# When to make the operand sums of a seven-product matmul: beside the transposes, or four pairs later

## The chip, the cores and the metric

One core of a Trainium2 chip runs the whole program in one launch. The metric is the device time of that launch in microseconds (us); lower is better. TensorE (PE) does the matrix products, VectorE (DVE) and ScalarE (ACT) the elementwise work, and SyncE (SP) issues the loads from HBM. Each of these executes its own instructions in a fixed order that is written when the program is built.

## The reference

A decoder trunk of two layers on 256 tokens of width 2048, all in float32. Each layer has attention and then a dense MLP with a hidden width of 8192:

```python
for layer in range(DEPTH):            # DEPTH = 2
    ...                               # projections, self- and memory attention
    h = layer_norm(ALPHA * h + mix, ln_g[layer, 0], ln_b[layer, 0])
    ffn = jnp.square(jax.nn.relu(h @ w_up[layer])) @ w_down[layer]
    h = layer_norm(ALPHA * h + ffn, ln_g[layer, 1], ln_b[layer, 1])
```

The change lies in the two products of the MLP.

## The kernel before

**Precision.** Every float32 operand is split into two parts, hi (`split`, L96, a cast on ACT) and lo (L97, a subtraction on DVE). One product of a 128-token block with a weight block of 128 x 512 takes three matmuls: hi by hi (L254), lo weights (L255) and lo tokens (L256).

**The MLP.** The hidden width is cut into four chunks of 2048. A chunk consists of two W_up groups (loop variable `v_`), then two W_down groups. A group (`mlp_group`) has 1024 output columns and a contraction over 2048 rows, which is taken as eight *pairs* of 128 rows in the order `ORDER = (2, 3, 0, 4, 1, 5, 6, 7)`. A pair needs one load of 1 MB. An ordinary pair is eight products, 24 matmuls. Pairs 0 and 1, which stand third and fifth in the order, are done with seven products instead (a Strassen-Winograd scheme), 21 matmuls. So a group is 6 x 24 + 2 x 21 = 186 matmuls.

Two groups are done another way, through `aform` and with eight products throughout: the first W_up group of the second layer, and in each layer the second W_down group of the last chunk. All eight second W_up groups (four chunks, two layers) go through `mlp_group`.

**What a seven-product pair needs.** On the weights' side `fast_weights` loads the pair, splits the blocks B11 and B22, and B21, and makes four sums T1 to T4 on DVE (L116, L119, L120), which are split too. On the tokens' side `fast_acts` makes four sums of the token blocks for pairs 0 and 1 at once: it adds hi and lo back together (L129), does four operations of 256 elements (L133 to L136), and splits the 1024 results (one cast on ACT into `sum_g` or `sum_h`, one subtraction on DVE). The sums for W_up (`sum_h`) are made once in a layer, those for W_down (`sum_g`) once in a chunk.

**Buffers.** The loaded weights, the tile t of the weights' sums and the tile `x_f` of the tokens' sums all rotate through four buffers of the tag "raw"; the hi parts have seven buffers of 1024 elements (tag "whi"), the lo parts seven others.

**Order around the change.** When a W_up group is complete, DVE adds the seven-product part, ACT does relu and square (L639 to L641), and the four 128 x 512 blocks must be transposed on PE (`transposed`: four small matmuls, an ACT cast L428, a DVE subtraction L429) to become the tokens of W_down, `gT`. These four transposes are hooks, emitted inside the next group at the places `UHOOKS = ((0, 3), (1, 0), (1, 2), (1, 3))`, where the first number counts pairs in order from 0 and the second the block of outputs within the pair. With the third of them both blocks of `gT0`, which holds the tokens of pairs 0 and 1, are complete, and there the kernel calls `fast_acts`:

```python
def back(b, v_=v_, us=us, gt=gt, sum_g=sum_g):
    transposed(us[b], gt[2 * v_ + b % 2], b // 2, 0)
    if v_ == 0 and b == 2:
        fast_acts(gt[0], sum_g)
```

So `sum_g` is emitted in the second pair of the second W_up group, just ahead of that group's first seven-product pair (the third in order). `sum_h` is emitted ahead of the layer's first `mlp_group`. The order of emission is what the framework's planner starts from when it writes each engine's order; it moves instructions ahead of others where it reckons that an engine is free.

Of the kernel before, what the change touches and what calls it, by code (L numbers as in the profile page):

```python
# [8 lines left out]
F32 = mybir.dt.float32  # L9
F32R = mybir.dt.float32r  # L10
I32 = mybir.dt.int32
AF = mybir.ActivationFunctionType
ALU = mybir.AluOpType
AX = mybir.AxisListType

P = 128
# [9 lines left out]
CH = 2048  # L26
# [7 lines left out]
NRAW = 4  # L34
# [30 lines left out]
WHOOKS = (10, 14, 4)  # L65
NWARM = 2
FILL = (10, 11, 12, 16)
ORDER = (2, 3, 0, 4, 1, 5, 6, 7)
FAST = (0, 1)
UHOOKS = ((0, 3), (1, 0), (1, 2), (1, 3))  # L70
WTAIL = ((1, 2), (2, 0), (3, 1), (5, 2), (7, 1), (9, 2))

# [2 lines left out]
def trunk(ctx: ExitStack, tc: tile.TileContext, a: dict, out: bass.AP):  # L75
    nc = tc.nc
    PS = bass.MemoryType.PSUM
    const = ctx.enter_context(tc.tile_pool(name="const", bufs=1))
    wp = ctx.enter_context(tc.tile_pool(name="wp", bufs=5))
    ap_ = ctx.enter_context(tc.tile_pool(name="act", bufs=1))  # L80
# [14 lines left out]
    def split(hi, lo, src):  # L95
        nc.scalar.copy(hi, src)  # L96
        nc.vector.tensor_tensor(lo, src, hi.bitcast(F32), ALU.subtract)  # L97
# [23 lines left out]
        pair(t_[:, 2:4].rearrange("p q c -> p (q c)"), 1024)  # L121
        return dict(zip(("B11", "B22", "B21", "T1", "T3", "T2", "T4"), tiles))

    def fast_acts(x, s_):


        raw = wp.tile([P, 2048], F32, name="x_f", tag="raw", bufs=NRAW)
        f = raw[:, :1024].rearrange("p (k t) -> p k t", k=4)
        nc.vector.tensor_tensor(f, x[:, :, 0].bitcast(F32), x[:, :, 1].bitcast(F32), ALU.add)  # L129
        a11, a21 = f[:, 0:4:2, :P], f[:, 0:4:2, P:]  # L130
        a12, a22 = f[:, 1:4:2, :P], f[:, 1:4:2, P:]
        s = raw[:, 1024:].rearrange("p (q u t) -> p q u t", q=4, u=2)
        nc.vector.scalar_tensor_tensor(s[:, 0], a21, -1.0, a22, op0=ALU.mult, op1=ALU.subtract)  # L133
        nc.vector.scalar_tensor_tensor(s[:, 1], s[:, 0], -1.0, a11, op0=ALU.mult, op1=ALU.subtract)
        nc.vector.tensor_tensor(s[:, 2], a11, a21, ALU.subtract)
        nc.vector.tensor_tensor(s[:, 3], a12, s[:, 1], ALU.subtract)  # L136
        split(s_[:, 0], s_[:, 1], raw[:, 1024:])

    def weights(src, parts=1):

# [91 lines left out]

        return ps, finish

    def mlp_group(src, xts, sums, hooks, early):

        ps = [ps_mm.tile([P, 512], F32, name="ps_g", tag="mm") for _ in range(4)]
        own = {}  # L240
        seen = {}
        last = {}
        plan = []
        for u in ORDER:
            plan.extend([(u, b) for b in range(4)] if u not in FAST else [(u, i) for i in range(7)])

        fast = ("P1", 0, 1, "P5", "P7", "P6", 2)
        for u in ORDER:
            for i in range(7 if u in FAST else 4):
                last[fast[i] if u in FAST else i] = (u, i)  # L250

        def mm3(bank, x, w, st, en):
            (xh, xl), (hi, lo) = x, w
            nc.tensor.matmul(bank, xh, hi, start=st, stop=False)  # L254
            nc.tensor.matmul(bank, xh, lo, start=False, stop=False)  # L255
            nc.tensor.matmul(bank, xl, hi, start=False, stop=en)  # L256

        def tok(k, t):
            return [xts[k // 4][:, k % 4, s, t * P:(t + 1) * P] for s in range(2)]

        left = len([u for u in ORDER if u in FAST])
        for pos, u in enumerate(ORDER):
            k0, k1 = 2 * u, 2 * u + 1
            if u in FAST:
                for i in range(4):
                    hooks.get((pos, i), nothing)()
                if not own:
                    for nm in ("P1", "P5", "P6", "P7"):
                        own[nm] = ps_at.tile([P, 512], F32, name=nm, tag="at")
                w = fast_weights(src[u])  # L270
                sx = [[sums[:, s, q, u % 2] for s in range(2)] for q in range(4)]
                prods = (("P1", tok(k0, 0), "B11"), (0, tok(k1, 0), "B21"), (1, sx[3], "B22"),
                         ("P5", sx[0], "T1"), ("P7", sx[2], "T3"), ("P6", sx[1], "T2"), (2, tok(k1, 1), "T4"))
                for i, (b, x, wn) in enumerate(prods):
                    mm3(own[b] if b in own else ps[b], x, w[wn], b not in seen, last[b] == (u, i))
                    seen[b] = True
                left -= 1
                if not left:
                    early(own)
                continue  # L280
            (h0, l0), (h1, l1) = weights(src[u])
            w = {"B11": (h0[:, :512], l0[:, :512]), "B22": (h0[:, 512:], l0[:, 512:]),
                 "B12": (h1[:, :512], l1[:, :512]), "B21": (h1[:, 512:], l1[:, 512:])}
            for b in range(4):
                hooks.get((pos, b), nothing)()
                t, n = b // 2, b % 2 + 1
                mm3(ps[b], tok(k0, t), w[f"B1{n}"], b not in seen, False)
                mm3(ps[b], tok(k1, t), w[f"B2{n}"], False, last[b] == (u, b))
                seen[b] = True
        return ps  # L290
# [191 lines left out]
    def sums_up(res):  # L482

        def early(own):
            u = [ap_.tile([P, 512], F32, name="u_n", tag="lg", bufs=NLG) for _ in range(4)]
            nc.scalar.copy(u[0], own["P1"])
            nc.vector.tensor_tensor(u[2], u[0], own["P6"], ALU.add)
            nc.vector.tensor_tensor(u[1], u[2], own["P5"], ALU.add)
            nc.vector.tensor_tensor(u[2], u[2], own["P7"], ALU.add)
            nc.vector.tensor_tensor(u[3], u[2], own["P5"], ALU.add)  # L490
            res.extend(u)
        return early
# [84 lines left out]
    hT = load_acts(a["xt"], "hT", "xT")  # L577
    h = []

    for l in range(LAYERS):  # L580
# [3 lines left out]
        v = evict_v(ps, "v")  # L584
# [29 lines left out]
        sum_h = None  # L614
        for c in range(FF // CH):
            gt = new_acts("og", "gT")
            todo = []
            sum_g = ap_.tile([P, 2, 4, 2, P], F32R, name="sum_g", tag="sum_g")
            for v_ in range(CH // 1024):

                hooks = dict(zip(UHOOKS, todo))
                us = [None] * 4
                if c == 0 and v_ == 0 and not more:
                    for nb in range(2):
                        ps, fin = aform([a["wup_s"][nb, i] for i in range(4)], hT, hold=(16 if nb == 0 else 0))
                        if nb == 0:
                            us[0] = relu2(ps[0])
                            fin()
                            us[2] = relu2(ps[1])
                        else:  # L630
                            us[1], us[3] = relu2(ps[0]), relu2(ps[1])
                else:
                    if sum_h is None:
                        sum_h = ap_.tile([P, 2, 4, 2, P], F32R, name="sum_h", tag="sum_h")
                        fast_acts(hT[0], sum_h)
                    acc = []
                    ps = mlp_group(a["wup"][l, c * (CH // 1024) + v_], hT, sum_h, hooks, sums_up(acc))
                    for b in range(4):
                        nc.vector.tensor_tensor(acc[b], acc[b], ps[b], ALU.add)  # L639
                        nc.scalar.activation(acc[b], acc[b], AF.Relu)  # L640
                        nc.scalar.activation(acc[b], acc[b], AF.Square)  # L641
                    us = acc

                def back(b, v_=v_, us=us, gt=gt, sum_g=sum_g):
                    transposed(us[b], gt[2 * v_ + b % 2], b // 2, 0)
                    if v_ == 0 and b == 2:
                        fast_acts(gt[0], sum_g)
                todo = [lambda b=b, f=back: f(b) for b in (0, 1, 2, 3)]
            last = c == FF // CH - 1
            if last and more:  # L650
                memt = load_acts(a["memt"], "hT", "memt")
            for v_ in range(D // 1024):
                if last and v_ == 1:
                    for nb in range(2, 4):
                        ps, fin = aform([a["wdn_s"][l, nb - 2, i] for i in range(4)], gt,
                                        hold=(0 if nb == 2 else 8 if more else HOLDF))
                        if nb == 2:
                            for t in range(NT):
                                residual(h, ps, t, nb, False, st)
                    continue  # L660
                ps = mlp_group(a["wdn"][l, v_, 8 * c:8 * c + 8], gt, sum_g, dict(zip(UHOOKS, todo)),
                               sums_down(h, v_, c == 0))
                todo = []
                for b in range(4):
                    residual(h, {b // 2: ps[b]}, b // 2, 2 * v_ + b % 2, False, st if last else None)
# [63 lines left out]
```

## Time and profile before

| | us |
|---|---|
| Median of 3 runs (2081.52 to 2083.8) | 2082.78 |
| The profiled execution, device time | 2085.73 |
| Its span, first to last instruction | 2083.6 |
| PE busy with matmuls in it | 2023.7 |

The profiled execution's time is 2.13 us more than its span and 2.95 us, 0.14%, above the median of the runs. A busy PE is not yet a PE at full clock: the granted clock is a column of its own in the profile, 1.00 being 2.4 GHz.

### The profile page before, as it was taken

The numbers are of one execution on the slowest core, as the hardware profiler recorded it, in microseconds if no ns is written. First come the engines' busy times: TensorE is split into PE (matmuls) and PEld (weight loads), VectorE is DVE, ScalarE is ACT, GpSimd is POOL, SyncE is SP. The second block draws the span as 40 slices with busy tenths as digits, with TensorE's granted clock in tenths as the row PEclk, the third lists the DMA queues.
The fourth block names the chain that finished last, engine by engine and source line by source line (L and its number), as shares of the span: only waits on it lengthen the run. The fifth ranks groups of instructions, "written<-read, shape, count | busy, mean of one in ns | idle before, by whom it ended". The sixth has DMA issues, their size and how long they took to land.

```text
span 2083.6 us, 23980 instructions
## 1 busy us (share of the span) xinstructions
PE 2023.7 (97%) x9326; PEld 1675.4 (80%) x9326; DVE 1540.2 (74%) x1951; ACT 1045.6 (50%) x1351; POOL 1.2 (0%) x8
## 2 busy tenths in 40 slices
PE   9999999999999999999999999999999999999997
PEld 7888888788778878878888888778887887888786
DVE  6566669688597868768885665769786876877785
ACT  5555535554464455456444554346445544654551
POOL 0000000000000000000000000000000000000000
PEclk9999999999999999999999999999999999999999
DMA  9644545455356545445754445425654554564562
GB/s 330 255 143 160 202 162 203 160 204 181 142 208 220 197 157 205 175 146 219 271 222 171 153 162 202 142 103 211 221 194 161 203 177 146 214 219 173 205 220 81
DMA packets 56273, 391.63 MB, mean 188 GB/s; under 512 B 6368, under 2 KB 6368, under 8 KB 9696
## 3 DMA queue, kind: packets, MB, share of 16 engines
q1 hardware_dynamic: 56160, 390.10, 52.1%
q8 instruction: 73, 1.20, 0.2%
q14 instruction: 40, 0.33, 0.0%
HBM read 387.98 MB, written 2.10 MB: 187 GB/s over the span
## 4 chain that ended last, share of the span: by engine, by line
PE 92%; DVE 6%; ACT 1%; issue 0%; DMA 0%; SPq 0%; DVEq 0%; ACTq 0%
PE ps_g L256 17%; PE ps_g L255 17%; PE ps_g L254 17%; PE ps_w L189 7%; PE ps_a L211 5%; PE ps_a L212 5%; PE ps_a L213 5%; PE ps_w L191 4%; PE P L254 3%; PE P L256 3%; PE P L255 3%; PE pt_h L426 2%; PE ps_m L536 1%; PE ps_m L538 1%; PE ps_m L537 1%; DVE h L419 1%
## 5 line engine op out<-in xcount | busy, mean ns | idle before, releaser
L97 DVE TENSOR_TENSOR wlo<-raw,whi 128x1024 fp32r<-128x1024 f32 (+1 forms) x706 | 815.7, 1174 | 329.0 <-ACT whi L96 324.9
L96 ACT CAST whi<-raw 128x1024 fp32r<-128x1024 f32 (+1 forms) x706 | 693.5, 1014 | 596.3 <-PE ps_g L256 323.6
L255 PE MATMUL ps_g<-wlo,hT 128*128 128x512 f32 x780 | 305.8, 392 | 0.1
L256 PE MATMUL ps_g<-whi,hT 128*128 128x512 f32 x780 | 305.9, 392 | 0.0
L254 PE MATMUL ps_g<-whi,hT 128*128 128x512 f32 x780 | 302.6, 395 | 0.9 <-ACT whi L96 0.7
L254 PE MATMUL ps_g<-whi,gT 128*128 128x512 f32 x728 | 285.3, 393 | 0.0
L256 PE MATMUL ps_g<-whi,gT 128*128 128x512 f32 x728 | 283.5, 390 | 0.0
L255 PE MATMUL ps_g<-wlo,gT 128*128 128x512 f32 x728 | 283.4, 390 | 0.0
L96 ACT CAST whi<-t 128x1024 fp32r<-128x1024 f32 x116 | 122.0, 1052 | 120.9 <-PE ps_g L256 45.0
L254 PEld LDWEIGHTS ps_g<-whi,hT 128*128 128x128 f32 x780 | 147.8, 190 | 33.7 <-ACT whi L96 3.8
L255 PEld LDWEIGHTS ps_g<-wlo,hT 128*128 128x128 f32 x780 | 147.7, 189 | 31.3 <-DVE wlo L97 0.5
L256 PEld LDWEIGHTS ps_g<-whi,hT 128*128 128x128 f32 x780 | 147.6, 189 | 31.0
L97 DVE TENSOR_TENSOR wlo<-t,whi 128x1024 fp32r<-128x1024 f32 x116 | 141.6, 1223 | 41.2 <-ACT whi L96 40.9
L256 PEld LDWEIGHTS ps_g<-whi,gT 128*128 128x128 f32 x728 | 136.7, 188 | 28.8
L255 PEld LDWEIGHTS ps_g<-wlo,gT 128*128 128x128 f32 x728 | 136.8, 188 | 27.6
L254 PEld LDWEIGHTS ps_g<-whi,gT 128*128 128x128 f32 x728 | 136.6, 188 | 27.2
L189 PE MATMUL ps_w<-hT,whi 128*128 128x512 f32 x320 | 119.9, 414 | 0.0
L189 PE MATMUL ps_w<-xT,whi 128*128 128x512 f32 x320 | 119.9, 414 | 0.0
L211 PE MATMUL ps_a<-whi,ot 128*128 128x512 f32 x256 | 101.7, 397 | 0.0
L213 PE MATMUL ps_a<-whi,ot 128*128 128x512 f32 x256 | 99.8, 390 | 0.0
L212 PE MATMUL ps_a<-wlo,ot 128*128 128x512 f32 x256 | 99.7, 389 | 0.0
L429 DVE TENSOR_TENSOR gT<-pt_h,gT 128x512 fp32r<-128x512 f32 x64 | 43.9, 688 | 67.0 <-ACT gT L428 67.0
(184 smaller groups left out, 2910.1 us busy)
## 6 DMA issues: line engine op xcount, KB each, us to landing
raw<-in_wup_dram SPq DMA_DIRECT2D x120, 1024.0 KB, 4.9
raw<-in_wdn_dram SPq DMA_DIRECT2D x112, 1024.0 KB, 4.9
raw<-in_wo_dram SPq DMA_DIRECT2D x32, 1024.0 KB, 4.8
raw<-in_wq_dram SPq DMA_DIRECT2D x24, 1024.0 KB, 4.8
raw<-in_wdn_s_dram SPq DMA_DIRECT2D x16, 1024.0 KB, 4.9
raw<-in_wmk_dram SPq DMA_DIRECT2D x8, 1024.0 KB, 6.2
raw<-in_wv_dram SPq DMA_DIRECT2D x8, 1024.0 KB, 7.3
raw<-in_wk_dram SPq DMA_DIRECT2D x8, 1024.0 KB, 4.8
```

What stands on the lines that cost most here:

```text
L96: nc.scalar.copy(hi, src)
L97: nc.vector.tensor_tensor(lo, src, hi.bitcast(F32), ALU.subtract)
L189: nc.tensor.matmul(ps, hi[:, kk:kk + P], x.rearrange("p s t -> p (s t)"), start=(k == 0), stop=False)
L191: nc.tensor.matmul(ps[:, :T], lo[:, kk:kk + P], x[:, 0], start=False, stop=(k == KT - 1))
L211: nc.tensor.matmul(ps[t], xh, hi, start=st, stop=False)
L212: nc.tensor.matmul(ps[t], xh, lo, start=False, stop=False)
L213: nc.tensor.matmul(ps[t], xl, hi, start=False, stop=en)
L254: nc.tensor.matmul(bank, xh, hi, start=st, stop=False)
L255: nc.tensor.matmul(bank, xh, lo, start=False, stop=False)
L256: nc.tensor.matmul(bank, xl, hi, start=False, stop=en)
L426: nc.tensor.transpose(pt[:, k], src[:, k * P:(k + 1) * P], ident)
L429: nc.vector.tensor_tensor(xt[:, :, 1, t * P:(t + 1) * P], pt, hi.bitcast(F32), ALU.subtract)
```

## The change

`fast_acts` becomes a generator with two steps. The first makes the sums (L129 to L136 of the old numbering, the same five DVE operations), the second splits them, now with one ACT cast and one DVE subtraction of 512 elements for each of the two pairs instead of one of 1024 for both. The steps are hooks of their own. For `sum_g` they are emitted at (5, 0) and (6, 0) of the second W_up group, its sixth and seventh pair, instead of beside the transpose at (1, 2). For `sum_h` they are emitted at (0, 0) and (1, 1) of the layer's first `mlp_group` instead of ahead of it. The sums' tiles are one for each pair now, and those of W_down lie in the tags "v" and "mk". The order of the pairs and the number of seven-product pairs (two of eight in W_up and in W_down) stay as they were.

```diff
-    def fast_acts(x, s_):
+    def fast_acts(xs, units):
...
+        parts = []
+        for j in range(0, len(units), 2):
+            n = len(units[j:j + 2])
+            x = xs[j // 2][:, :2 * n]
+            raw = wp.tile([P, 2, 8, P], F32, name="x_f", tag="raw", bufs=NRAW)
+            f = raw[:, 0, :4 * n].rearrange("p (k t) c -> p k (t c)", t=2)
+            nc.vector.tensor_tensor(f, x[:, :, 0].bitcast(F32), x[:, :, 1].bitcast(F32), ALU.add)
...
+            parts += [s[:, u] for u in range(n)]
+        yield
+        for (hi, lo), s in zip(units, parts):
+            split(hi, lo, s)
+        yield
...
-            sum_g = ap_.tile([P, 2, 4, 2, P], F32R, name="sum_g", tag="sum_g")
+            sum_g = sum_units(DOWN[1], ("v", "mk"))
...
-                        fast_acts(hT[0], sum_h)
+                        sum_h = sum_units(UP[1], ("sum_h0", "sum_h1", "pts"))
+                        steps = fast_acts(hT, sum_h)
+                        hooks[0, 0] = hooks[1, 1] = lambda s=steps: next(s)
+                    if v_ == 1:
+                        steps = fast_acts(gt, sum_g)
+                        hooks[5, 0] = hooks[6, 0] = lambda s=steps: next(s)
...
-                def back(b, v_=v_, us=us, gt=gt, sum_g=sum_g):
+                def back(b, v_=v_, us=us, gt=gt):
                     transposed(us[b], gt[2 * v_ + b % 2], b // 2, 0)
-                    if v_ == 0 and b == 2:
-                        fast_acts(gt[0], sum_g)
```

## Rows read from the trace of the kernel before

**Rows 1.** The page, busy time by engine: us, share of span, instructions.
```profile
PE 2023.7 (97%) x9326; PEld 1675.4 (80%) x9326; DVE 1540.2 (74%) x1951; ACT 1045.6 (50%) x1351; POOL 1.2 (0%) x8
```

**Rows 2.** Waits of PE, whole run: us in total, times, longest.
```profile
PE P L254 <- ACT whi L96: 38.3, 16, 3.5
PE pt_h L426 <- DVE h L420: 3.7, 2, 2.0
```

**Rows 3.** Windows: W_down half of chunk one, then W_up halves of chunks two, three.
```profile
427.18:513.39 86.21, 86.21 (x389) 71.39 (x388) 73.47 (x83) 44.28 (x51) 0.00 (x0) 1.00 0.55 195
513.39:608.03 94.64, 89.84 (x390) 73.14 (x388) 68.42 (x76) 49.72 (x60) 0.00 (x0) 0.96 0.49 178
694.24:788.88 94.64, 89.82 (x389) 73.09 (x388) 68.39 (x76) 49.53 (x60) 0.00 (x0) 0.96 0.49 177
```

**Rows 4.** Windows of 16 us around the sums, first and last of eight.
```profile
384.00:400.00 16.00, 11.20 (x40) 8.18 (x39) 12.53 (x16) 7.87 (x10) 0.00 (x0) 0.79 0.20 66
...
1941.00:1957.00 16.00, 11.19 (x37) 8.09 (x36) 13.22 (x17) 8.39 (x11) 0.00 (x0) 0.79 0.55 205
```

**Rows 5.** Timeline of the first of them: start, us, engine, line, operation, [idle before].
```profile
385.87 1.22 DVE L129 TENSOR_TENSOR x_f<-gT 128x1024 f32<-128x1024 f32 x1
...
386.36 0.59 ACT L428 CAST gT<-pt_h 128x512 fp32r<-128x512 f32 x1 [1.25 <-PE pt_h L426]
...
387.32 0.40 PE L256 MATMUL ps_g<-whi,hT 128*128 128x512 f32 x1
...
388.73 0.43 DVE L136 TENSOR_TENSOR x_f<-x_f 128x256 f32<-128x256 f32 x1
389.19 1.04 ACT L96 CAST sum_g<-x_f 128x1024 fp32r<-128x1024 f32 x1 [2.24 <-DVE x_f L136]
390.14 1.56 ACT L96 CAST whi<-raw 128x1024 fp32r<-128x1024 f32 x2
...
391.24 0.50 PE L254 MATMUL P<-whi,hT 128*128 128x512 f32 x1 [3.51 <-ACT whi L96]
...
393.76 0.80 PE L254 MATMUL P<-whi,sum_h 128*128 128x512 f32 x1 [1.27 <-ACT whi L96]
...
395.21 0.63 PE L255 MATMUL ps_g<-wlo,hT 128*128 128x512 f32 x1
...
395.64 0.63 PE L256 MATMUL ps_g<-whi,hT 128*128 128x512 f32 x1
```

**Rows 6.** Timeline of DVE in the first W_down group of chunk one.
```profile
427.98 1.22 DVE L116 TENSOR_TENSOR t<-raw 128x1024 f32<-128x1024 f32 x1
...
432.52 0.69 DVE L429 TENSOR_TENSOR gT<-pt_h,gT 128x512 fp32r<-128x512 f32 x1 [0.25 <-ACT gT L428]
...
450.79 2.36 DVE L97 TENSOR_TENSOR wlo<-raw,whi 128x1024 fp32r<-128x1024 f32 x2 [3.49 <-ACT whi L96]
...
453.66 1.22 DVE L97 TENSOR_TENSOR wlo<-raw,whi 128x1024 fp32r<-128x1024 f32 x1
...
457.13 1.22 DVE L97 TENSOR_TENSOR wlo<-raw,whi 128x1024 fp32r<-128x1024 f32 x1
```

**Rows 7.** Groups of DVE's instructions in the 122 us from 348 us, by form.
```profile
L97 DVE TENSOR_TENSOR wlo<-raw,whi 128x512 fp32r<-128x512 f32 x5 | 3.4, 685 | 0.0
```

**Rows 8.** Waits of PE between 300 and 340 us.
```profile
PE ps_g L254 <- ACT whi L96: 0.7, 1, 0.7
```

**Rows 9.** Timeline of ACT ahead of the second layer's first second-W_up group.
```profile
1388.06 1.28 ACT L518 ACTIVATE u_n<-ps_a 128x512 f32<-128x512 f32 x2 [6.38 <-PE ps_a L213]
```

**Rows 10.** A window in the layer norm of the second layer.
```profile
1336.00:1340.00 4.00, 3.40 (x15) 2.64 (x16) 3.86 (x6) 1.72 (x3) 0.00 (x0) 0.76 1.01 397
```

**Rows 11.** SP's own waits, whole run.
```profile
SPq L104 <- DVE sum_g L97: 144.3, 8, 21.9
```

**Rows 12.** Timeline of SP, the first two loads of the next W_down group.
```profile
409.75 3.19 SPq L145 DMA_DIRECT2D raw<-in_wdn_dram  x2
```

**Rows 13.** The page, DMA issues: count, KB, us from issue to landing.
```profile
raw<-in_wdn_dram SPq DMA_DIRECT2D x112, 1024.0 KB, 4.9
```

More of the change, by code (lines that the diff above doesn't have):

```diff
@@ L67 @@
 FILL = (10, 11, 12, 16)
-ORDER = (2, 3, 0, 4, 1, 5, 6, 7)
-FAST = (0, 1)
+UP = ((2, 3, 0, 4, 1, 5, 6, 7), 2)
+DOWN = ((2, 3, 0, 4, 1, 5, 6, 7), 2)
 UHOOKS = ((0, 3), (1, 0), (1, 2), (1, 3))
@@ L122, in fast_weights @@
         return dict(zip(("B11", "B22", "B21", "T1", "T3", "T2", "T4"), tiles))
-    def fast_acts(x, s_):
[L127 to L137, printed above, removed]
+    def fast_acts(xs, units):
[6 more added lines that the diff above has]
+            nc.vector.tensor_tensor(f, x[:, :, 0].bitcast(F32), x[:, :, 1].bitcast(F32), ALU.add)
+            a11, a21 = f[:, 0:2 * n:2, :P], f[:, 0:2 * n:2, P:]
+            a12, a22 = f[:, 1:2 * n:2, :P], f[:, 1:2 * n:2, P:]
+            s = raw[:, 1, :4 * n].rearrange("p (u q) c -> p u q c", q=4)
+            nc.vector.scalar_tensor_tensor(s[:, :, 0], a21, -1.0, a22, op0=ALU.mult, op1=ALU.subtract)
+            nc.vector.scalar_tensor_tensor(s[:, :, 1], s[:, :, 0], -1.0, a11, op0=ALU.mult, op1=ALU.subtract)
+            nc.vector.tensor_tensor(s[:, :, 2], a11, a21, ALU.subtract)
+            nc.vector.tensor_tensor(s[:, :, 3], a12, s[:, :, 1], ALU.subtract)
+            parts += [s[:, u] for u in range(n)]
[3 more added lines that the diff above has]
+        yield
@@ L139, in weights, with sum_units @@
+    def sum_units(n, tags):
+        units = []
+        for tag in tags[:n]:
+            if tag == "pts":
+                units.append([ap_.tile([P, 4, P], F32R, name="sums", tag="pts", bufs=2) for _ in range(2)])
+            else:
+                t_ = ap_.tile([P, 2, 4, P], F32R, name="sums", tag=tag)
+                units.append([t_[:, s] for s in range(2)])
+        return units
     def weights(src, parts=1):
@@ L233, in aform, with mlp_group @@
         return ps, finish
-    def mlp_group(src, xts, sums, hooks, early):
+    def mlp_group(src, xts, sums, hooks, early, order, nfast):
         ps = [ps_mm.tile([P, 512], F32, name="ps_g", tag="mm") for _ in range(4)]
@@ L242, in mlp_group @@
         last = {}
-        plan = []
-        for u in ORDER:
-            plan.extend([(u, b) for b in range(4)] if u not in FAST else [(u, i) for i in range(7)])
         fast = ("P1", 0, 1, "P5", "P7", "P6", 2)
-        for u in ORDER:
-            for i in range(7 if u in FAST else 4):
-                last[fast[i] if u in FAST else i] = (u, i)
+        for u in order:
+            for i in range(7 if u < nfast else 4):
+                last[fast[i] if u < nfast else i] = (u, i)
         def mm3(bank, x, w, st, en):
@@ L259, in tok @@
             return [xts[k // 4][:, k % 4, s, t * P:(t + 1) * P] for s in range(2)]
-        left = len([u for u in ORDER if u in FAST])
-        for pos, u in enumerate(ORDER):
+        left = nfast
+        for pos, u in enumerate(order):
             k0, k1 = 2 * u, 2 * u + 1
-            if u in FAST:
+            if u < nfast:
                 for i in range(4):
@@ L270, in mlp_group @@
                 w = fast_weights(src[u])
-                sx = [[sums[:, s, q, u % 2] for s in range(2)] for q in range(4)]
+                sx = [[s[:, q] for s in sums[u]] for q in range(4)]
                 prods = (("P1", tok(k0, 0), "B11"), (0, tok(k1, 0), "B21"), (1, sx[3], "B22"),
@@ L633, in trunk @@
                     if sum_h is None:
-                        sum_h = ap_.tile([P, 2, 4, 2, P], F32R, name="sum_h", tag="sum_h")
-                        fast_acts(hT[0], sum_h)
+                        sum_h = sum_units(UP[1], ("sum_h0", "sum_h1", "pts"))
[4 more added lines that the diff above has]
+                        hooks[5, 0] = hooks[6, 0] = lambda s=steps: next(s)
                     acc = []
-                    ps = mlp_group(a["wup"][l, c * (CH // 1024) + v_], hT, sum_h, hooks, sums_up(acc))
+                    ps = mlp_group(a["wup"][l, c * (CH // 1024) + v_], hT, sum_h, hooks, sums_up(acc), *UP)
                     for b in range(4):
@@ L661, in trunk @@
                 ps = mlp_group(a["wdn"][l, v_, 8 * c:8 * c + 8], gt, sum_g, dict(zip(UHOOKS, todo)),
-                               sums_down(h, v_, c == 0))
+                               sums_down(h, v_, c == 0), *DOWN)
                 todo = []
```

## The prediction

> **What bounds the kernel now.** I read the page first. PE is busy for 97% of the span, DVE for 74% [rows 1]; so PE sets the time, and what is to be had is PE's idle time and the time it runs at less than full clock. PE's own waits come second: nearly all of them are one kind, the first matmuls of a seven-product pair waiting for a hi cast on ACT, 38.3 us in 16 waits [rows 2]. To see where, I cut the MLP into halves of chunks. Two W_up groups and two W_down groups hold the same work: 2 x 186 = 372 large matmuls and 16 small transposes each, 388, and the windows count 389 and 390. The W_down half takes 86.21 us, at a granted clock of 1.00 and with PE busy throughout. The W_up half takes 94.64 us, at 0.96, in two different chunks to the hundredth [rows 3]. The difference, 8.43 us, is the loss, and it is measured against a half that has the same transposes and the same seven-product pairs but no token sums in it. The eight windows around the sums of the eight chunks look alike, PE busy 11.2 of 16 us at 0.79 [rows 4], so the loss is there eight times.
>
> The timeline says how it comes about. The addition of hi and lo (L129) can start only at 385.87, when the third transpose has arrived. The last transpose's ACT cast begins at 386.36 and takes 0.59. PE's last matmul of the second pair starts at 387.32. ACT's next instruction in its order is the cast of the token sums, and it stands idle for 2.24 us until DVE has made them, at 389.19. Behind it in the same order stands the cast of the next pair's weights, at 390.14, and PE's first product of the seven-product pair waits for that: 3.51 us idle, to 391.24, then 1.27 us more until T1 and T3 are cast [rows 5]. The raw weights are not what is late; the queue order is. Idle is 4.78 us of the 8.43; the other 3.65 us are matmuls at the lower clock, 1.2 GHz (395.21 to 395.64, a step of 0.43 us [rows 5], where the whole undisturbed half averages 86.21 / 372 = 0.232 us for each large matmul, transposes included).
>
> **The change, part by part.**
>
> *The token sums leave the second pair.* Behind the last transposes ACT can then go straight to the weights' casts, and DVE to T1 to T4. How far the planner would bring those forward the trace of before shows in the first W_down group, which has the four transposes at the same places and no sums: DVE makes the third pair's weight sums at 427.98, ahead of even the first transpose's subtraction at 432.52 [rows 6], and the half has no PE idle. I take that as the model for the second W_up group. Gain: 8 x 8.43 = 67.4 us.
>
> *The same work arrives at the sixth and seventh pair.* DVE: 1.22 us for L129 and four operations like the one of 0.43 [rows 5], together 2.9 us, then two subtractions of 512 at 0.685 [rows 7], 1.4 us. ACT: two casts that cannot take longer than two of the present 1.04 us [rows 5]. The tokens have been there since the second pair, so nothing here waits for PE. The cover is DVE's lead. In the W_down group, which starts at 427.18, PE reaches the seventh pair after 114 + 24 large matmuls, 427.18 + 138 x 0.232 = 459.2, and the eighth at 464.7. Counting the halves of the splits, DVE has finished the seventh pair's at 453.66 + 1.22 = 454.9 and the eighth's at 457.13 + 1.22 = 458.4 [rows 6]: leads of 4.3 and 6.4 us. The sums take 2.9 us ahead of the seventh pair and 4.3 ahead of the eighth. Both fit, with 1.4 and 2.1 us over, and DVE's 3.49 us of idle time just before [rows 6] is not even counted. As a whole half: DVE busy 68.4 us now [rows 3], and 68.6 of 86.2 afterwards, less than the 73.5 of 86.2 with which the W_down half keeps PE fed. If the cover were gone, the price would be up to 4.3 us a chunk, 34 us in all.
>
> *One split of 1024 becomes two of 512.* Two take 2 x 0.685 = 1.37 us [rows 7] where one of 1024 takes 1.22 [rows 6], some 0.15 us more of DVE ten times over: 1.5 us if nothing hid it, nothing under the leads above. The Trainium skill (VectorE: DVE Perf Modes, "The TRN2 errata") speaks against such cutting: an SBUF operation pays a fixed cost per instruction, so few large ones beat many small ones. Its table's 58 cycles at 0.96 GHz would be an estimate of 0.06 us for each of the ten extra instructions, 0.6 us; the rows give 1.5, and the sum uses neither.
>
> *The sums of W_up* move from ahead of the layer's first group to its first two pairs. The weights' splits of the first pair now come first; the 0.7 us that PE waits for one of them there [rows 8] may go. Against that 4.3 us of DVE work stands nearer to the third pair, but it is work that DVE did just before, so the end of the chain does not move by more than the extra 0.15 us. I take -0.7 us in the first layer, bounds -0.7 and +4.3, and nothing in the second, where ACT has 6.38 us of idle time to spare ahead of that group [rows 9].
>
> *The buffers.* Moving the tiles to other tags adds no wait that I can find: "v" and "mk" are read for the last time in the attention, and again only in the next layer. `x_f` still takes one of four "raw" buffers; that is a rival below.
>
> *Sum.* 2085.73 - 67.4 - 0.7 = 2017.6 for the profiled execution; the median is 2.95 us below that execution, so 2014.7. I add some 1.3 us for small waits where DVE and PE meet at the sixth to eighth pair, which I cannot bound better than by the 34 us above: **2016 us**.
>
> **The rivals.**
>
> *The cast still comes late (partial gain).* For it: in the second layer's first chunk ACT had 6.38 us with nothing to do [rows 9] and no cast of the third pair was put there, so the order on the queue is not simply "whatever is ready". If the planner leaves the third pair's casts behind the last transpose, they start at 386.36 + 0.59 = 386.95 and not at 390.14, 3.19 us earlier, and idle falls from 4.78 to 1.59. Whether the clock holds through that is open: a stretch with 0.60 us of PE idle and small transposes ran at 0.76 [rows 10]. So 3.2 to 6.8 us a group are saved, 26 to 55 us: 2028 to 2057 us. Against it: rows 6.
>
> *The sums' buffer holds back the loads (slower).* `x_f` is one of four buffers in turn. Now the load that follows in its place waits for the sums eight times, 144.3 us, 18.0 on average and 21.9 at most [rows 11]. After the change it would be the second load of the W_down group. Now it is issued by 412.94 [rows 12], and that pair is wanted 24 x 0.232 = 5.6 us after 427.18, 19.8 us later. Landing takes 4.9 us [rows 13] and the cast 1.04, so a wait of up to 13.9 us is free. With the lost clock it turns the change into a loss where 3.65 + (wait - 13.9) exceeds 8.43, beyond 18.7 us; at 21.9 us it costs 3.2 us net a chunk, 26 us: 2108 us. Against it: the waits of before were long because the sums waited for transposes on PE, and these wait for nothing.
>
> *Nothing changes* (2083), if the planner brings the sums forward to the transposes again, since their tokens are complete there and DVE has idle time. Unlikely: emitted at the sixth pair, they have the weights' splits of three more pairs ahead of them in line.
>
> **How the numbers follow.** The forecast case, the loss gone: 0.76, with a range of its own of 2010 to 2026. The partial gain: 0.16. Nothing: 0.03. Slower: 0.05. The range reaches from 2010 (all small terms in favour) to 2043, the middle of the partial case's 2028 to 2057; that leaves out half of 0.16, the 0.08 of the last two, and a little of the first. Faster by over 0.2% (which is about what a measurement of this kernel can tell from no change): 0.92. Within: 0.03. Slower: 0.05.
>
> **What would show it.** The W_up half at 86 to 87 us with clock 1.00 and no PE idle in it; PE's wait total for ACT near zero; DVE's sum operations between the splits of the sixth to eighth pairs; SP's loads in even steps through the half. Wrong if PE waits appear at the third pair again (the partial case), at the sixth to eighth (DVE's lead was too small), or at the second pair of the W_down group behind a late load (the buffer).

## The result and the profile after

The changed kernel takes 2015.72 us (median of 4 runs, 2014.11 to 2016.56) against 2082.6 (four runs, one more than the table ahead of the prediction has; 2081.52 to 2083.8): a ratio of 0.9678, 95% interval 0.9661 to 0.9695, or 66.9 us less. The forecast was 2016. Lines of `kernel.py` are those of the new numbering from here on: L97 is the cast, L98 the subtraction of a split, L135 to L142 the token sums, L445 and L446 a transpose's cast and subtraction, L105 a seven-product pair's load and L165 an ordinary one's.

The page of the changed kernel, busy time by engine, beside [rows 1]:

```profile
PE 1994.2 (99%) x9326; PEld 1662.3 (83%) x9326; DVE 1543.9 (77%) x1961; ACT 1046.0 (52%) x1361; POOL 1.2 (0%) x8
```

The matmuls are the same in number. PE's waits in the whole run, beside [rows 2]:

```profile
PE pt_h L443 <- DVE h L437: 4.2, 2, 2.2
PE ps_m L553 <- ACT whi L97: 2.0, 1, 2.0
PE ps_warm L94 <- DVE warm L91: 1.5, 1, 1.5
```

The 38.3 us in 16 waits for a hi cast at a seven-product pair are gone, all of them, and so is the 0.7 us of [rows 8]. What is left lies in the layer norms and at the start. Now the halves of chunks, beside [rows 3], and a window of 16 us around the start of the third pair, beside [rows 4] (length, then the busy time of PE, weight loads, DVE, ACT and POOL, granted clock, DMA share, GB/s):

```profile
416.58:502.83 86.25, 86.25 (x390) 71.40 (x388) 71.35 (x80) 44.41 (x52) 0.00 (x0) 1.00 0.55 195
502.83:589.09 86.26, 86.26 (x390) 71.41 (x388) 71.02 (x80) 49.43 (x61) 0.00 (x0) 1.00 0.54 196
```
```profile
379.70:395.70 16.00, 16.00 (x76) 13.25 (x75) 13.19 (x17) 8.51 (x12) 0.00 (x0) 1.00 0.52 181
```

The W_up half costs 86.26 us, 8.38 less than before, and to 0.01 us what the W_down half costs. DVE's share of it is 71.0 of 86.3.

How the queues stand now, from the timeline of ACT and then of DVE in the second W_up group of the first chunk, whose third pair PE begins at 385.30:

```profile
375.19 1.04 ACT L97 CAST whi<-t 128x1024 fp32r<-128x1024 f32 x1
377.25 0.59 ACT L445 CAST gT<-pt_h 128x512 fp32r<-128x512 f32 x1 [1.02 <-PE pt_h L443]
...
384.80 2.69 ACT L97 CAST whi<-raw 128x1024 fp32r<-128x1024 f32 x3
...
394.89 0.62 ACT L97 CAST sums<-x_f 128x512 fp32r<-128x512 f32 x1 [3.57 <-DVE x_f L142]
...
398.75 0.61 ACT L97 CAST sums<-x_f 128x512 fp32r<-128x512 f32 x1
```
```profile
389.90 1.22 DVE L135 TENSOR_TENSOR x_f<-gT 128x1024 f32<-128x1024 f32 x1
...
395.55 0.69 DVE L98 TENSOR_TENSOR sums<-x_f,sums 128x512 fp32r<-128x512 f32 x1 [0.69 <-ACT sums L97]
...
396.50 3.61 DVE L98 TENSOR_TENSOR wlo<-raw,whi 128x1024 fp32r<-128x1024 f32 x3 [0.26 <-ACT whi L97]
...
400.62 0.69 DVE L98 TENSOR_TENSOR sums<-x_f,sums 128x512 fp32r<-128x512 f32 x1
...
403.55 1.22 DVE L98 TENSOR_TENSOR wlo<-raw,whi 128x1024 fp32r<-128x1024 f32 x1
```

The cast of weight sums (`whi<-t`) at 375.19 is the third pair's, and it stands ahead of the first transpose's cast, as in the W_down group of [rows 6]. Before, the first cast of this pair came at 390.14, behind all four transposes and the token sums [rows 5]. The token sums run from 389.90 to 401.3, while PE is in the third to sixth pairs. ACT waits 3.57 us for them, longer than the 2.24 of before, and it costs nothing: what PE needs next was cast long ago.

### The profile page after: what moved, and what is told of

It reads as the page before. It is cut to its first block, busy times and chain, and to the rows that moved or that the text cites. A ratio compares the mean times of both kernels' runs of the same rounds, so it can differ in the third digit from the quotient of the medians.

```text
span 2014.4 us, 23998 instructions
## 1 busy us (share of the span) xinstructions
PE 1994.2 (99%) x9326; PEld 1662.3 (83%) x9326; DVE 1543.9 (77%) x1961; ACT 1046.0 (52%) x1361; POOL 1.2 (0%) x8
## 4 chain that ended last, share of the span: by engine, by line
PE 96%; DVE 3%; issue 0%; DMA 0%; ACT 0%; SPq 0%; DVEq 0%
PE ps_g L271 18%; PE ps_g L273 18%; PE ps_g L272 18%; PE ps_w L209 7%; PE ps_a L231 5%; PE ps_a L232 5%; PE ps_a L233 5%; PE ps_w L211 4%; PE P L271 3%; PE P L273 3%; PE P L272 3%; PE pt_h L443 2%; PE ps_m L553 1%; PE ps_m L554 1%; PE ps_m L555 1%; DVE h L436 1%
## 5 line engine op out<-in xcount | busy, mean ns | idle before, releaser
L98 DVE TENSOR_TENSOR wlo<-raw,whi 128x1024 fp32r<-128x1024 f32 (+1 forms) x706 | 818.1, 1174 | 329.7 <-ACT whi L97 325.2
L97 ACT CAST whi<-raw 128x1024 fp32r<-128x1024 f32 (+1 forms) x706 | 697.2, 1014 | 624.5 <-PE ps_g L273 349.7
L273 PE MATMUL ps_g<-whi,hT 128*128 128x512 f32 x780 | 303.8, 390 | 0.0
L272 PE MATMUL ps_g<-wlo,hT 128*128 128x512 f32 x780 | 303.7, 389 | 0.0
L273 PE MATMUL ps_g<-whi,gT 128*128 128x512 f32 x728 | 283.7, 390 | 0.0
L272 PE MATMUL ps_g<-wlo,gT 128*128 128x512 f32 x728 | 283.4, 389 | 0.0
L273 PEld LDWEIGHTS ps_g<-whi,hT 128*128 128x128 f32 x780 | 146.4, 188 | 30.8
L272 PEld LDWEIGHTS ps_g<-wlo,hT 128*128 128x128 f32 x780 | 146.6, 188 | 29.3
L273 PEld LDWEIGHTS ps_g<-whi,gT 128*128 128x128 f32 x728 | 136.7, 188 | 28.9
L97 ACT CAST whi<-t 128x1024 fp32r<-128x1024 f32 x116 | 122.0, 1052 | 72.5 <-PE ps_g L273 45.1
L272 PEld LDWEIGHTS ps_g<-wlo,gT 128*128 128x128 f32 x728 | 136.8, 188 | 27.3
L98 DVE TENSOR_TENSOR wlo<-t,whi 128x1024 fp32r<-128x1024 f32 x116 | 141.5, 1222 | 20.9 <-ACT whi L97 20.5
L211 PE MATMUL ps_w<-xT,wlo 128*128 128x256 f32 x320 | 89.9, 281 | 0.0
```

Of the source, the lines that this page charges most:

```text
L211: nc.tensor.matmul(ps[:, :T], lo[:, kk:kk + P], x[:, 0], start=False, stop=(k == KT - 1))
```

## Experiments

Each kernel was timed against the kernel before, whose median in these comparisons was 2082.99 to 2083.29 us. Diffs are against the changed kernel unless another is named.

**The two moves apart.** First, only the W_up sums at their new place:

```diff
-                    if v_ == 1:
-                        steps = fast_acts(gt, sum_g)
-                        hooks[5, 0] = hooks[6, 0] = lambda s=steps: next(s)
...
+                    if v_ == 0 and b == 2:
+                        for _ in fast_acts(gt, sum_g):
+                            pass
```

> The changed kernel, but with the sums for W_down made where they were, with the third transpose of the second W_up group; only the sums for W_up stand at their new place. If the 67 us come from the W_down sums alone, as the prediction has it, the W_up half takes about 94.6 us again, PE waits some 38 us for hi casts in 16 waits, and the time is 2081 us (1.4 us of the 69 stay, at the first group of the first layer). If the move of the W_up sums had a larger part in it, the time would be clearly below 2078 us.

Measured: 2078.09 us, ratio 0.9976 (0.9967 to 0.9986). The waits of PE, and the windows of the W_up half and of the stretch around its stall:

```profile
PE P L271 <- ACT whi L97: 28.8, 8, 3.6
PE P L272 <- DVE wlo L98: 4.9, 8, 0.9
```
```profile
509.13:603.47 94.34, 89.88 (x390) 73.07 (x388) 68.43 (x77) 49.68 (x61) 0.00 (x0) 0.96 0.49 179
```
```profile
384.00:387.50 3.50, 0.00 (x0) 0.00 (x0) 2.78 (x7) 2.06 (x4) 0.00 (x0) 1.00 0.00 0
387.50:392.00 4.50, 4.02 (x9) 2.49 (x9) 4.49 (x5) 1.59 (x3) 0.00 (x0) 0.56 0.66 233
392.00:396.00 4.00, 4.00 (x13) 3.21 (x12) 2.87 (x3) 3.25 (x4) 0.00 (x0) 0.64 0.00 0
396.00:400.00 4.00, 4.00 (x20) 3.29 (x19) 4.00 (x5) 1.49 (x3) 0.00 (x0) 1.00 0.95 354
```

The loss is back: the half at 94.34 us, a wait of 3.6 us in each of eight groups, and then 8.5 us at 0.56 to 0.64 of the clock for which the rows list 9 and 13 large matmuls, where the next 4 us have 20 (one on an edge counts in both rows). So the sums for W_down carry nearly all of the gain. The run is 3 us faster than expected: the second wait is now for a lo part, 0.6 us on average, where it was 1.27 [rows 5]. This kernel still has the finer split of the change, and that may be why; the cut was not tried by itself.

Then the other half, only the W_down sums moved:

```diff
-                        steps = fast_acts(hT, sum_h)
-                        hooks[0, 0] = hooks[1, 1] = lambda s=steps: next(s)
+                        for _ in fast_acts(hT, sum_h):
+                            pass
```

> The other half: the W_down sums at their new place, the W_up sums made ahead of the layer's first group as before. Expected 2017 us, with the 0.7 us wait of PE for a hi cast back at the first group of the first layer and the W_up half at 86.3 us. If the two moves lean on each other, a wait comes back in the second layer's first second-W_up group and the time is 2025 us or more.

Measured: 2017.15 us, ratio 0.9683 (0.967 to 0.97), 1.43 us above the full change. The one wait that came back is that of the first group, as in [rows 8], a little longer:

```profile
PE ps_g L271 <- ACT whi L97: 1.1, 1, 1.1
```

**Is it the place?** The prediction took the place beside the transposes for the cause. Four kernels ask. The first leaves the sums there, as the first run did, and gives their tile a buffer of its own (diff against the first run):

```diff
-            raw = wp.tile([P, 2, 8, P], F32, name="x_f", tag="raw", bufs=NRAW)
+            raw = ap_.tile([P, 2, 8, P], F32, name="x_f", tag="x_f")
```

> As the first of these runs, sums at the old place beside the third transpose, but the tile of the sums has a buffer of its own and no longer takes a turn among the four of the loaded weights. Place theory (the sums' cast stands in ACT's queue ahead of the third pair's casts because it is emitted there): nothing changes, 2081 us, W_up half 94.6 us. Buffer theory (the third pair's loads and weight sums come behind the sums' tile in the ring of four, so the planner cannot bring their casts forward ahead of the sums): most of the loss goes, 2016 to 2030 us, W_up half 86 to 88 us, and the casts of the third pair's weights stand ahead of the sums on ACT.

Measured: 2015.93 us, ratio 0.9677 (0.9663 to 0.9691): the whole gain, with the sums where they always were. The W_up half, and ACT's timeline in the second W_up group:

```profile
503.03:589.29 86.26, 86.26 (x390) 71.40 (x388) 70.71 (x80) 49.21 (x61) 0.00 (x0) 1.00 0.53 196
```
```profile
374.77 1.03 ACT L97 CAST whi<-t 128x1024 fp32r<-128x1024 f32 x1
...
384.30 0.59 ACT L445 CAST gT<-pt_h 128x512 fp32r<-128x512 f32 x1 [1.25 <-PE pt_h L443]
385.00 2.69 ACT L97 CAST whi<-raw 128x1024 fp32r<-128x1024 f32 x3
...
388.70 1.14 ACT L97 CAST sums<-x_f 128x512 fp32r<-128x512 f32 x2
```

The third pair's weight sums are cast at 374.77, ahead of the transposes, and the casts of the sums follow at 388.70, behind the transposes. Nothing was emitted later; the planner was free to bring the weights forward. (The buffer of its own lies in another pool, `ap_` and not `wp`; a tag of its own in the same pool was not tried.) The second and third kernels of the four move the sums to the start of the third pair, behind the last transpose but ahead of that pair's weights, and to the start of the fourth:

```diff
-                        hooks[5, 0] = hooks[6, 0] = lambda s=steps: next(s)
+                        hooks[2, 0] = lambda s=steps: [next(s), next(s)]
```

(for the other, `hooks[3, 0]`).

> The changed kernel with both steps of the W_down sums emitted at the start of the third pair, just behind the last transpose and still ahead of the third pair's weights. If it is being beside the transposes that costs, this is late enough and the time is near 2016 us. If it is being ahead of the third pair's weights, in the queues and in the ring of buffers, the loss stays: some 2080 us, W_up half 94 to 95 us.

> Both steps at the start of the fourth pair, behind the third pair's weights and between the two seven-product pairs, where DVE has most to do. If it only matters to be behind the third pair's weights: 2016 us, as at the sixth and seventh pair. If DVE's lead is too short there for 4.3 us more, PE waits at the fifth pair, up to 4 us a chunk, 32 us in all: up to 2050 us.

Measured: 2077.91 us at the third pair (ratio 0.9977, 0.9967 to 0.9986) and 2015.29 at the fourth (0.9675, 0.966 to 0.9689). Their W_up halves:

```profile
508.95:602.57 93.62, 89.63 (x389) 72.71 (x388) 68.45 (x77) 49.67 (x61) 0.00 (x0) 0.96 0.48 180
```
```profile
502.08:588.34 86.26, 86.26 (x389) 71.41 (x388) 70.71 (x80) 49.01 (x60) 0.00 (x0) 1.00 0.53 196
```

Away from the transposes is not enough. Behind the third pair's weights is, and the sixth and seventh pair are no better than the fourth, where DVE was thought to have least to spare. The fourth kernel asks whether ACT's queue alone is at fault. Sums at the old place and in the ring, their hi cast made on DVE (for the W_up sums too); against the first run:

```diff
-            split(hi, lo, s)
+            nc.vector.tensor_copy(hi, s)
+            nc.vector.tensor_tensor(lo, s, hi.bitcast(F32), ALU.subtract)
```

> As the first run, sums at the old place and in the ring, but their hi cast is a copy on DVE, so ACT never waits for the sums. If ACT's queue is what makes PE idle, the first wait of 3.5 us goes to under 1 us and the time falls to some 2040 us or lower; DVE has some 1.2 us more to do ahead of T1 to T4, so the second wait of 1.3 us stays or grows. If DVE's chain is just as late (transposes, sums, then T1 to T4 in one queue), PE waits as long as before in total and the time is 2080 us or more.

Measured: 2077.79 us, ratio 0.9974 (0.9964 to 0.9983). The waits of PE, and of the timeline the first casts and the first lo parts of the third pair (behind the edit this kernel's lines are one higher, so L272 is hi by hi and L273 lo weights):

```profile
PE P L273 <- DVE wlo L98: 34.2, 8, 4.3
...
PE P L272 <- ACT whi L97: 1.8, 8, 0.2
```
```profile
383.57 1.57 ACT L97 CAST whi<-raw 128x1024 fp32r<-128x1024 f32 x2
...
387.80 1.22 DVE L117 TENSOR_TENSOR t<-raw 128x1024 f32<-128x1024 f32 x1
...
388.93 1.82 DVE L98 TENSOR_TENSOR wlo<-raw,whi 128x1024 fp32r<-128x1024 f32 x2
```

With ACT freed from the sums, the cast of the third pair's weights follows the last transpose at once, at 383.57, and the first wait does shrink, to 0.2 us. But DVE has the same order of work, sums first, and the pair's lo parts come at 388.93; PE waits 4.3 us for them. So the theory of ACT's queue fails as stated: both queues held the third pair's work behind the sums.

**Is it the number of buffers or the turn?** Two kernels, both with the sums at the old place. In the first the ring has five buffers, with the sums' tile in it (against the first run); in the second the sums' tile has its own buffer and the ring has three (against the third kernel above):

```diff
-NRAW = 4
+NRAW = 5
```
```diff
-NRAW = 4
+NRAW = 3
```

> Sums at the old place beside the third transpose and their tile in the ring of the loaded weights, but that ring has five buffers and not four (the room is what the old sums' tile left). Number theory (with the sums' tile in it four buffers are one too few): most of the loss goes, 2016 to 2030 us. Turn theory (what counts is that the third pair's tiles take their turn behind the sums' tile, however many there are): the loss stays, 2070 us or more.

> The sums' tile in a buffer of its own, sums at the old place, and only three buffers left for the loaded weights and their sums. It parts the same two theories from the other side. Number theory: with three buffers the third pair's work is held up as before, 2070 us or more. Turn theory: the third pair's casts can still go ahead of the token sums; three buffers make the loads later, which may cost something of its own in every group, but the waits in the second W_up group are not longer than in the others: 2016 to 2050 us.

Measured: five buffers 2078.16 us (ratio 0.9977, 0.9967 to 0.9986), three 2016.95 (0.9681, 0.9666 to 0.9695). More buffers do not help while the sums' tile is among them; fewer do no harm once it is not. With five, from the timelines of SP (the first row the third pair's load, the second the fifth's) and of ACT, and PE's waits:

```profile
357.70 0.33 SPq L105 DMA_DIRECT2D raw<-in_wup_dram  x1
...
368.04 0.33 SPq L105 DMA_DIRECT2D raw<-in_wup_dram  x1
```
```profile
386.02 1.14 ACT L97 CAST sums<-x_f 128x512 fp32r<-128x512 f32 x2 [2.24 <-DVE x_f L142]
387.07 1.56 ACT L97 CAST whi<-raw 128x1024 fp32r<-128x1024 f32 x2
```
```profile
PE P L271 <- ACT whi L97: 28.8, 8, 3.6
PE P L272 <- DVE wlo L98: 5.4, 8, 0.9
```

The third pair's load is issued at 357.70, some 29 us before its cast at 387.07, and even the fifth pair's load no longer waits for the sums. The data are there and ACT stands idle for 2.24 us just before; in the run with the sums' cast on DVE the same cast runs right behind the last transpose's, at 383.57. So it is the written order that holds it back. What counts, then, is the turn in the ring: while the sums' tile has its turn ahead of the third pair's tiles, the planner writes that pair's casts and lo parts behind the sums.

**How much cover there is.** The sums done three times over at the sixth pair; two of the three results are not used:

```diff
+                        def thrice(s, gt=gt, sum_g=sum_g):
+                            for more_s in (fast_acts(gt, sum_g), fast_acts(gt, sum_g)):
+                                next(more_s), next(more_s)
+                            next(s)
...
-                        hooks[5, 0] = hooks[6, 0] = lambda s=steps: next(s)
+                        hooks[5, 0] = lambda s=steps: thrice(s)
+                        hooks[6, 0] = lambda s=steps: next(s)
```

> The changed kernel with the W_down sums' work done three times over at the sixth pair (two further runs of all its operations, with tiles of their own from the same ring, then the one that counts), to see how much cover there is. It adds 8.6 us of DVE work and 2.5 us of ACT work a chunk. If the leads of 4.3 and 6.4 us and the 3.5 us of idle time that the prediction counted were all the cover, PE waits some 1 to 4 us a chunk: 2024 to 2048 us. If the planner spreads the work over the whole half, where DVE would be busy 79.6 of 86.3 us, it costs nothing: 2016 us.

Measured: 2020.77 us, ratio 0.9701 (0.9687 to 0.9716), 5.1 us above the change or 0.6 a chunk, below the range of the one theory and above the other's. PE's waits in the first layer's MLP, and ten microseconds of a second W_up group:

```profile
PE ps_g L271 <- ACT whi L97: 1.1, 1, 1.1
PE ps_g L272 <- DVE wlo L98: 0.8, 1, 0.8
```
```profile
560.00:570.00 10.00, 10.00 (x46) 8.29 (x45) 10.00 (x14) 5.63 (x8) 0.00 (x0) 1.00 0.00 0
```

DVE is full and no load moves in those ten microseconds, and PE stays busy. The waits in the rows explain 1.9 of the 5.1 us; where the rest goes is left open.

**Is there a better version?** The change leaves `mlp_group` free to do more than two pairs with seven products. Three in W_up, three in both, and three in W_up with five buffers in the ring (the third diff against the first):

```diff
-UP = ((2, 3, 0, 4, 1, 5, 6, 7), 2)
+UP = ((3, 4, 0, 5, 1, 6, 2, 7), 3)
```
```diff
-UP = ((2, 3, 0, 4, 1, 5, 6, 7), 2)
-DOWN = ((2, 3, 0, 4, 1, 5, 6, 7), 2)
+UP = ((3, 4, 0, 5, 1, 6, 2, 7), 3)
+DOWN = ((3, 4, 0, 5, 1, 6, 2, 7), 3)
...
-            sum_g = sum_units(DOWN[1], ("v", "mk"))
+            sum_g = sum_units(DOWN[1], ("v", "mk", "sum_g2"))
```
```diff
-NRAW = 4
+NRAW = 5
```

> A candidate: three of eight pairs with seven products in the W_up groups, in the order 3, 4, 0, 5, 1, 6, 2, 7. It saves 3 matmuls of 0.227 us in each of 15 groups, 10.2 us: 2005.5 us if DVE keeps up. DVE gets some 4.2 us more for each of these groups and would be busy about 79.5 of 86.3 us of a W_up half. If it cannot keep up, PE waits at the fifth to seventh pair and the gain is lost: 2016 us or more.

> A candidate: three pairs of eight with seven products in W_down too (order 3, 4, 0, 5, 1, 6, 2, 7 for both). Against the three in W_up alone it saves 0.68 us in each of 14 groups, 9.5 us: 1999 us if DVE keeps up. DVE would be busy some 80 of 85 us of a W_down half, and the residual additions come on top at the group ends, so PE may wait there: 2009 us or more if it does.

> A candidate: three seven-product pairs in W_up, sums at the new places, five buffers in the ring of loaded weights. If the 3 us that the three pairs fell short of 2005.5 are late loads or the sums' tile in the ring, 2005 us; if DVE's own time is what is short, 2008 us as with four.

Measured: 2008.64 us with three in W_up (ratio 0.9644, 0.9629 to 0.9658), 2018.94 with three in both (0.9691, 0.9677 to 0.9706), 2005.22 with three in W_up and five buffers (0.9626, 0.9612 to 0.964). The last is the best, and its interval lies wholly below that of the change. PE's waits with three in W_up and four buffers, and with three in both:

```profile
PE pt_h L443 <- ACT u_n L662: 2.0, 3, 0.9
```
```profile
PE ps_a L232 <- DVE wlo L98: 5.1, 2, 2.6
PE pt_h L443 <- ACT u_n L662: 5.1, 7, 1.7
...
PE ps_g L271 <- ACT whi L97: 1.8, 7, 0.5
```

The 2.0 us are absent with five buffers, where the 10.2 us of the expectation arrive whole (2015.72 - 2005.22 = 10.5). With three in both, PE waits for transposes behind relu and square, and for lo parts of the pairs that follow; DVE is then busy for 83% of the span, as the page has it. What exactly makes it 10 us slower than three in W_up alone was not taken apart.

## Why the prediction was right

**The size.** Point by point: 8 x 8.43 = 67.4 us was forecast for the W_down sums, and the half went from 94.64 to 86.26, 8 x 8.38 = 67.0. Reading the loss as the difference between two halves with the same matmuls, rather than as the 38.3 us of waits, is what made the number: waits alone would have given less than 0.6 of it, since the slow clock behind them is not counted as waiting. The first layer's first group was put at -0.7, and the second run puts it at 1.43 by the medians (the runs of one kernel scatter by as much) with a wait of 1.1 us in its rows. The 1.3 us kept back for small waits at the sixth to eighth pair were not needed. In the profiled executions the sum is 67.0 + 1.4 = 68.4 of 2085.73 - 2016.56 = 69.2 us; the rest is about the 0.86 us of the first load of the program, 4.86 us in the chain against 5.72, which the change does not touch. That the forecast came within 0.3 us is luck. Misses of some 2.5 us in one direction (the 1.3 kept back, 0.7 at the first group, 0.86 at the first load, less 0.4 at the W_down sums) met one of 2.1 us in the other: the profiled execution lay 2.95 us above the median before, as the forecast assumed for after too, but 0.84 after.

**The model.** That the second W_up group would come to look like the first W_down group, weights ahead of transposes [rows 6], is what the timeline after shows.

**The cover.** The leads were right in kind, and larger than forecast. In DVE's order the four operations and the first split of the sums stand between the halves of the sixth pair's splits, and the second split stands between the seventh pair's and the eighth's, much as I had written; only the first addition stands earlier, among the fifth pair's. DVE as a whole runs ahead of PE: by the timeline after, counting the halves, it has finished the seventh pair's at 396.50 + 3.61 = 400.1 and the eighth's at 403.55 + 1.22 = 404.8, and PE begins these pairs later:

```profile
405.70 0.39 PE L271 MATMUL ps_g<-whi,hT 128*128 128x512 f32 x1
...
411.14 0.39 PE L271 MATMUL ps_g<-whi,hT 128*128 128x512 f32 x1
```

That is 5.6 and 6.4 us with the sums done, where the prediction had 1.4 and 2.1 left over. DVE's busy time in the half, put at 68.6 us, measured 71.0: the weight sums of the next group's third pair, 1.22 + 2 x 0.69 us, are now made inside it, from 408.81 on in the first chunk, where before they came at 427.98, behind the end of the half at 427.18 [rows 3, rows 6]. Emission at the fourth pair does as well, and three times the work costs 0.6 us a chunk.

**What failed is the step that said why.** The prediction has "The raw weights are not what is late; the queue order is", and that stands. But it put the order down to the place beside the transposes and, in the first place, to ACT's queue. Neither holds: behind the last transpose no more is gained than at the old place (2077.91 against 2078.09), at the old place the whole gain comes (2015.93) if the sums' tile is out of the ring, and with ACT out of it DVE's queue costs as much (2077.79). Moving the sums worked because it moved their tile's turn behind the third pair's. The trace of before had a sign of it in [rows 9], which I counted for the partial-gain rival: ACT stood idle for 6.38 us with that pair's load issued at 1375.89, and cast nothing. By which rule the planner lets a turn in the ring hold back a cast whose data are loaded and whose own buffer is another one, the runs do not show; that stays open.

**The rivals.** The late load did not come up. SP's waits for the sums, beside [rows 11]:

```profile
SPq L165 <- DVE sums L98: 12.5, 2, 11.7
SPq L105 <- DVE sums L98: 5.2, 7, 0.8
```

The wait of 11.7 us is that of a load behind the W_up sums, in the first layer's first group. The loads behind the W_down sums wait eight times, at most 0.8 us each, far below the 13.9 worked out as free. Seven of them are a seven-product pair's (L105): the sums' buffer goes to the third load of the W_down group, not to the second as the prediction had it. The eight waits of 18.0 us on average were long because those sums waited for the transposes [rows 5]. The partial gain did not come up.

**The finer split.** The prediction weighed the fixed cost of cutting one split into two at up to 1.5 us. The run with the cut and without the move came out 3 us below its expectation instead. The Trainium skill (Perfetto Trace Analysis, "Optimizing Scalar/DVE Operations") has the opposite advice for engines that are not full but cause bubbles elsewhere: break instructions up, so that work completes sooner. The shorter second wait in that run agrees with it, 0.6 us against 1.27, though the cut by itself was not measured.

## What to carry to other kernels

When an engine is idle beside data that are loaded, look at which tiles share a ring of buffers: a tile that must wait for a late event can hold back, by its turn alone, the work of the tiles behind it, and a fifth buffer in the ring did not cure that here; a buffer of its own, or a later turn, did. To size a stall, compare the stretch with an undisturbed one of the same work instead of adding up waits, because the slow clock that follows an idle stretch can cost three quarters as much again (here 3.65 us behind 4.78). And when a gain arrives as forecast, still undo the parts one by one: the number was right here and half of the reason was not.

## What the runs showed of the hardware

In the run with the W_down sums at the old place the granted clock reads 1.00 through the 3.5 us in which PE does nothing, and falls to means of 0.56 and 0.64, so mostly the lower level of 1.2 GHz, only in the 8.5 us after, when it works again; the drop is paid by the matmuls behind the gap. Single waits of PE of 1.1 us (only the W_down sums moved) and 0.8 us (the sums done three times) left the granted clock of the windows around them at 1.00. In the kernel before, a wait of PE of 2.0 us [rows 2] ended at 1336.58, and the stretch from 1336 to 1340 us shows 0.76 [rows 10].
